# Layer 1 feed forward: every second gate and up block from the fifth on as seven block products, with all their sums and splits on DVE

## The chip, the cores and the metric

One NeuronCore of a Trainium2 chip runs the whole program. The metric is the device time of one execution in microseconds (us). The engines are PE (TensorE, matmuls; PEld is its weight load), DVE (VectorE), ACT (ScalarE), POOL (GpSimd) and SP (SyncE, which here issues the DMAs). Each engine executes its own instructions in a fixed order and waits on semaphores for the others.

## What is computed

A two-layer diffusion block on 512 latent tokens and 256 context tokens, width 1024. The change lies in the feed forward of the second layer (layer 1), which runs on the 512 latent tokens alone:

```python
def conv_ffn(h, w_up, conv_w, conv_b, w_down):
    g, u = jnp.split(h @ w_up, 2, axis=-1)
    g = dwconv(g, conv_w) + conv_b
    return (jax.nn.silu(g) * u) @ w_down
...
x_lat = x_lat + g1 * y_lat
x_lat = x_lat + g2 * conv_ffn(rmsnorm(x_lat, norm_ffn[layer]) * (1 + sc2) + sh2, *ffn_p[layer])
```

`w_up` is 1024 x 5632, that is 22 gate blocks and 22 up blocks of 128 columns; `w_down` is 2816 x 1024. `dwconv` is a convolution of three taps along the tokens.

## The kernel before

Activations lie transposed: 128 features on the partitions, tokens along the free axis. Every product is done in three passes of a rounded type: an operand is split into a high half (a cast on ACT) and a low half (source minus high, on DVE); this is `split` (lines 98 to 100). `gemm` (line 123) then issues for each of the 8 slices of the contraction high x high, high x low and low x high, and a matmul has its own weight load. A block f of the feed forward is one gate and one up block: 2 x 8 x 3 = 48 matmuls of 128x512.

`ffn` (line 1016) handles one block after the other, in groups of 8, 8 and 6 (`GROUPS`). For each block it loads the gate and up weights (`load_wk`: a DMA of 512 KB into a `raw` tile, a cast into `wh` on ACT, a subtraction into `wl` on DVE, each 128x1024), multiplies them into two PSUM tiles, and finishes with the convolution (`conv`, line 497: an ACT activation and two DVE instructions L96 of 128x511), Silu on ACT (L1041), the product with up (L93 on DVE) and a split. After a group come its eight down projections (`project`, line 929), the last group's through `passes` (line 939), which also prepares the final norm.

What sets the order: a scheduler places the instructions of each engine by the program's order, its own estimate of durations, and free buffers. The rings of buffers matter here: `raw`, `wh` and `wl` two buffers each, PSUM tiles `g` two buffers of 1024 columns (so the gate tile of block n+1 takes the buffer of the gate tile of block n, once the convolution has read it), `m` three, `t` five, `u` four, `ada` two. In block 1 the gate weights lie in slots of their own (`hold`), so that they can be split before block 0 is done.

Block 0 is multiplied in two halves of 256 tokens, because the norm before it (`norm_seg`, line 217 ff., with `norm_apply`) comes in two halves: per half and 8 slices it makes the high half on ACT and the low half on DVE (even slices) or POOL (odd slices), after a product of x with the scale, which reads PSUM.

Of the kernel before, what the change touches and what calls it, by code (L numbers as in the profile page):

```python
# [8 lines left out]
F32 = mybir.dt.float32  # L9
F32R = mybir.dt.float32r  # L10
# [40 lines left out]
def hybrid_kernel(ctx: ExitStack, tc: tile.TileContext, A, out):  # L51
# [204 lines left out]
    def ada_raw():  # L256
        return ap.tile([P, 1024], F32, tag="ada", name=nm("ada"))
# [681 lines left out]
    def passes(src, nk, mv, layer, which, segs, acc, norm):  # L939
        for m in range(KD - 2):  # L940
            project(load_wk(src(m), nk), mv, layer, which, m, segs, acc)
        w = [load_wk(src(m), nk) for m in (KD - 2, KD - 1)]
        apply = None
        for seg in segs:
            for i in range(2):
                project(w[i], mv, layer, which, KD - 2 + i, (seg,), acc)
            nxt = norm(seg)
            if apply:
                apply()
            apply = nxt  # L950
        return apply
# [334 lines left out]
            x[3 * i + k] = s[:, k, :]  # L1286
    acc = temp()[:, :NL]
    a, b = mod_ab(1, 1, "norm_ffn_1", 1)
    h = new_h((0, 1, 20, 21, 4, 6, 11, 15))
    apply = passes(lambda m: A["w_o"][m], KD, oh, 1, 0, HALF, acc, lambda seg: norm_seg(x, acc, a, b, h, seg))  # L1290
    acc2 = temp()[:, :NL]
    fn = vec("final_norm")

# [19 lines left out]

        return apply

    def tail_1(src, ng, acts):
        return passes(src, ng, acts, 1, 1, HALF, acc2, final)

    apply = ffn(1, h, zs, LAT, HALF, apply, tail_1, (7, 8, 9, 10, 18, 19, 16, 17, 5, 2), (18, 19))
    apply()  # L1320


# [146 lines left out]
```

## Time and profile before

| what | value |
|---|---|
| runs, median (lowest to highest) | 1777.81 us (1776.45 to 1781.27), 3 runs |
| the profiled execution | 1776.61 us |
| its span, first to last instruction | 1774.8 us |
| mean granted TensorE clock | 0.984 of full |
| PE / DVE / ACT / POOL busy | 97% / 61% / 37% / 11% of the span |
| the layer-1 feed forward, first matmul of block 0 to the last down projection | about 1384 to 1757 us |

The profiled execution lies 1.2 us under the median of the runs. 1.8 us of it are outside the span. Times in the rows are counted from the start of the span.

### The profile page before, as it was taken

What the parts mean: (1) busy time and instruction counts of PE and PEld (TensorE: products, weight loads), DVE (VectorE), ACT (ScalarE), POOL (GpSimd) and SP (SyncE); (2) the same over time, 40 slices, a digit from 0 to 9 for tenths busy, and PEclk for the clock granted to TensorE, in tenths of its full rate; (3) what the DMA queues carried; (4) which work ended last, traced back from release to release, by engine and by line L of the source; (5) the groups of instructions that cost most, each with busy time, mean ns of one, the idle gap of its engine ahead of it and who ended that gap; (6) DMA issues with size and microseconds to landing.
All of it is one profiled execution on the core that took longest, in us unless ns stands there. A gap on an engine that the chain in (4) does not pass through costs nothing.

```text
span 1774.8 us, 24363 instructions
## 1 busy us (share of the span) xinstructions
PE 1715.9 (97%) x9615; PEld 1439.0 (81%) x9615; DVE 1089.2 (61%) x1871; ACT 651.3 (37%) x1091; POOL 192.5 (11%) x193
## 2 busy tenths in 40 slices
PE   8899999998999999999999999989999999999997
PEld 2578887887888888888888888978888888888886
DVE  6777866739967457764355436487884644344445
ACT  4542332446543321132211324455553432232233
POOL 1551242015213000000000000000000300000001
PEclk9899999998999999999999999999999999999998
DMA  7156455312523134553255123110022223233322
GB/s 273 60 175 207 150 189 187 125 58 71 179 84 108 60 107 131 178 156 99 79 172 170 62 63 116 36 35 27 26 100 72 72 95 95 95 96 95 95 83 84
DMA packets 65668, 193.59 MB, mean 109 GB/s; under 512 B 7086, under 2 KB 17136, under 8 KB 65554
## 3 DMA queue, kind: packets, MB, share of 16 engines
q1 hardware_dynamic: 65554, 192.03, 33.5%
q8 instruction: 76, 1.25, 0.3%
q14 instruction: 38, 0.31, 0.1%
HBM read 178.37 MB, written 13.63 MB: 108 GB/s over the span
## 4 chain that ended last, share of the span: by engine, by line
PE 68%; DVE 4%; ACT 1%; POOL 1%; issue 1%; DVEq 0%; ACTq 0%; POOLq 0%
PE g L128 60%; PE g L1208 3%; PE m L128 1%; PE m L1226 1%; DVE t L93 1%; PE a L104 1%; PE a L103 1%; PE a L105 1%; DVE s L100 1%; DVE wl L100 0%; PE m L206 0%; PE a L128 0%; PE m L217 0%; POOL t L242 0%; PE a L321 0%
## 5 line engine op out<-in xcount | busy, mean ns | idle before, releaser
L128 PE MATMUL g<-s,wh 128*128 128x512 f32 (+1 forms) x4464 | 1077.7, 349 | 9.4 <-ACT s L241 3.6
L128 PEld LDWEIGHTS g<-s,wh 128*128 128x128 f32 x4464 | 727.5, 189 | 131.0 <-issue 6.6
L128 PE MATMUL g<-s,wl 128*128 128x512 f32 (+2 forms) x2232 | 655.4, 348 | 0.1
L99 ACT CAST wh<-raw 128x1024 fp32r<-128x1024 f32 (+4 forms) x219 | 213.4, 974 | 667.9 <-PE g L128 586.6
L128 PEld LDWEIGHTS g<-s,wl 128*128 128x128 f32 x2232 | 369.1, 189 | 58.0 <-DVE wl L100 0.6
L100 DVE TENSOR_TENSOR wl<-raw,wh 128x1024 fp32r<-128x1024 f32 (+4 forms) x219 | 251.0, 1148 | 232.8 <-ACT wh L99 227.6
L96 DVE SCALAR_TENSOR_TENSOR acc<-ada,sc,acc 128x512 f32<-128x512 f32 x224 | 164.9, 775 | 30.3 <-DMA ada<-in_ada_dram 28.8
L96 DVE SCALAR_TENSOR_TENSOR s<-g,mod,s 128x512 f32<-128x512 f32 (+1 forms) x102 | 62.5, 632 | 147.9 <-PE g L128 147.5
L96 DVE SCALAR_TENSOR_TENSOR t<-g,vecs,t 128x511 f32<-128x511 f32 x204 | 131.0, 642 | 26.5 <-ACT t L501 20.6
L93 DVE TENSOR_TENSOR t<-t,g 128x768 f32<-128x768 f32 (+2 forms) x52 | 41.3, 794 | 110.0 <-PE g L128 109.2
L501 ACT ACTIVATE t<-g,vecs 128x512 f32<-128x512 f32 x86 | 59.9, 696 | 79.4 <-DVE t L96 62.7
L242 POOL TENSOR_SCALAR t<-t,A,mod 128x256 f32<-128x256 f32 (+1 forms) x36 | 37.5, 1048 | 376.8 <-DVE t L93 372.8
L1208 PE MATMUL g<-s,s 128*128 128x512 f32 (+1 forms) x320 | 65.4, 347 | 3.7 <-DVE s L93 2.5
L1208 PEld LDWEIGHTS g<-s,s 128*128 128x128 f32 x320 | 49.3, 190 | 10.9 <-DVE s L93 4.1
L1041 ACT ACTIVATE t<-t 128x768 f32<-128x768 f32 (+1 forms) x42 | 31.1, 740 | 68.5 <-DVE t L96 68.5
L100 DVE TENSOR_TENSOR s<-m,s 128x512 fp32r<-128x512 f32 (+1 forms) x90 | 50.2, 588 | 8.3 <-ACT s L99 8.0
L99 ACT CAST s<-m 128x512 fp32r<-128x512 f32 (+1 forms) x90 | 42.5, 515 | 34.0 <-PE m L1226 24.1
L1308 POOL TENSOR_TENSOR s<-s,t 128x256 f32<-128x256 f32 x8 | 5.5, 728 | 363.1 <-ACT t L1304 363.1
L1151 POOL MEMSET s<- 64x768 f32 x1 | 0.7, 734 | 398.6 <-PE g L128 398.6
L199 ACT ACTIVATE t<-s 128x256 f32<-128x256 f32 (+2 forms) x58 | 31.4, 561 | 21.6 <-DVE s L96 18.1
L1217 ACT ACTIVATE u<-g,mx 128x768 f32<-128x768 f32 x32 | 28.9, 905 | 25.3 <-DVE mx L1215 23.0
L100 DVE TENSOR_TENSOR s<-t,s 128x768 fp32r<-128x768 f32 (+1 forms) x44 | 36.0, 818 | 0.0
(363 smaller groups left out, 1858.0 us busy)
## 6 DMA issues: line engine op xcount, KB each, us to landing
raw<-in_up_dram SPq DMA_DIRECT2D x88, 512.0 KB, 3.5
ada<-in_ada_dram SPq DMA_DIRECT2D x82, 512.0 KB, 3.7
raw<-in_down_dram SPq DMA_DIRECT2D x32, 512.0 KB, 3.6
raw<-in_w_in_dram SPq DMA_DIRECT2D x24, 512.0 KB, 4.5
raw<-in_w_out_dram SPq DMA_DIRECT2D x16, 512.0 KB, 3.4
s<-in_ada_dram SPq DMA_DIRECT2D x14, 512.0 KB, 7.9
s<-in_xT_dram SPq DMA_DIRECT2D x8, 768.0 KB, 5.5
raw<-in_down_dram SPq DMA_DIRECT2D x16, 384.0 KB, 3.2
```

Of the source, the lines that this page charges most:

```text
L93: return dve.tensor_tensor(o, a, b, op=op)
L96: return dve.scalar_tensor_tensor(o, a, s, b, op0=op0, op1=op1)
L99: act.copy(h, src)
L100: eng.tensor_tensor(l, src, f32(h), op=ALU.subtract)
L103: pe.matmul(o, s[0], m[0], start=start, stop=False)
L128: pe.matmul(ps[r][:, :n] if type(ps) is list else ps[:, lo:lo + n], w[a][:, k - k0, :], mv[k][b][:, lo:lo + n], start=first and k == ks[0] ...
L199: act.activation(sq, xa, AF.Square)
L242: pool.tensor_scalar(f[:, s], t[:, s], a[i], b[i], op0=ALU.mult, op1=ALU.add)
L501: act.activation(d, s, AF.Identity, scale=w[:, 1:2], bias=bias)
L1041: act.activation(t[:, :n], t[:, :n], AF.Silu, **({} if f else dict(bias=zs)))
L1208: pe.matmul(g[:, lo:lo + w_], s_, m_[:, lo:lo + w_], start=n == 0, stop=n == 4)
L1217: act.activation(pt, g[:, :T], AF.Exp, scale=MLA_SCALE, bias=mx, accum_out=sm)
```

## The change

Block 0 to 3, every odd block, 20 and 21 stay as they were, with 48 matmuls of 512 columns. Blocks 4, 6, 8, 10, 12, 14, 16 and 18 (eight of them) go through the new function `seven` (after.py, lines 1401 to 1442). The weights of up and gate form a 2 x 2 matrix of pieces (a11, a12 the two contraction halves of up; a21, a22 those of gate), and the activations one too (contraction halves by token halves of 256). Instead of eight products of pieces there are seven, each of 4 slices x 3 passes = 12 matmuls of 128x256. For that, four sums of weight pieces (`s1` to `s4`, 128x512 on DVE) are made per block; all seven weight operands are split from there (`wform`: cast of 128x512 on ACT, subtraction of 128x512 on DVE, in the buffers of `wh` and `wl`), and seven additions of 128x256 on DVE and one copy on ACT put gate and up together in SBUF. The raw weights come into the `ada` buffers.

Four sums of the activations are needed once for all blocks: `token_forms` computes them from the unsplit activations F (4 slices x 4 sums, 128x256 on DVE) and splits them (16 casts on ACT, 16 subtractions on DVE). So `norm_half` replaces `norm_seg`: it also writes F, on ACT for the even slices, on POOL for the odd ones.

```diff
-    h = new_h((0, 1, 20, 21, 4, 6, 11, 15))
-    apply = passes(lambda m: A["w_o"][m], KD, oh, 1, 0, HALF, acc, lambda seg: norm_seg(x, acc, a, b, h, seg))
+    us = [slot(i, [P, 6, NC], F32R) for i in (0, 1, 20, 21, 4, 6, 11, 15)]
...
+        def apply():
+            for k in range(KD):
+                t = temp()[:, :NC]
+                tt(t, x[k][:, s], g, ALU.mult)
+                hi, lo = B[k][j]
+                ak, bk = a[:, k, 0:1], b[:, k, 0:1]
+                act.activation(hi, t, AF.Identity, scale=ak, bias=bk)
+                if k % 2:
+                    pool.tensor_scalar(F[j][k], t, ak, bk, op0=ALU.mult, op1=ALU.add)
+                else:
+                    act.activation(F[j][k], t, AF.Identity, scale=ak, bias=bk)
+                (pool if k % 2 else dve).tensor_tensor(lo, F[j][k], f32(hi), op=ALU.subtract)
...
+    def token_forms():
+        for k in range(4):
+            f11, f12, f21, f22 = F[0][k], F[1][k], F[0][k + 4], F[1][k + 4]
+            t = temp()
+            t1, t2 = t[:, 0:NC], t[:, NC:2 * NC]
+            tt(t1, f12, f11, ALU.subtract)
+            tt(t2, f22, t1, ALU.subtract)
+            tt(f12, f22, f12, ALU.subtract)
+            tt(f21, f21, t2, ALU.subtract)
+            for n, v in enumerate((t1, t2, f12, f21)):
+                split(TF[n][k][0], TF[n][k][1], v)
...
-    apply = ffn(1, h, zs, LAT, HALF, apply, tail_1, (7, 8, 9, 10, 18, 19, 16, 17, 5, 2), (18, 19))
+    def wform(src, eng=dve):
+        t = wp.tile([P, 2, 512], F32R, tag=("wh", "wl")[turn[0] % 2], name=nm("wf"))
+        turn[0] += 1
+        split(t[:, 0, :], t[:, 1, :], src, eng)
+        return [t[:, i, :].rearrange("p (k m) -> p k m", m=P) for i in range(2)]
+
+    def seven(f):
...
+        tt(s1, a21, a22, ALU.add)
+        tt(s2, s1, a11, ALU.subtract)
+        product(p1, wform(a11), B11)
+        act.copy(q1, p1)
+        product(p6, wform(s2), T2)
+        tt(q6, p6, q1, ALU.add)
+        product(p5, wform(s1), T1)
+        tt(us_[:, hi], p5, q6, ALU.add)
+        product(p2, wform(a12), B21)
+        tt(us_[:, lo], p2, q1, ALU.add)
+        tt(s3, a11, a21, ALU.subtract)
+        product(p7, wform(s3), T3)
+        tt(q67, p7, q6, ALU.add)
+        tt(gs_[:, hi], p5, q67, ALU.add)
+        product(p4, wform(a22), T4)
+        tt(gs_[:, lo], p4, q67, ALU.add)
+        tt(s4, a12, s2, ALU.subtract)
+        product(p3, wform(s4), B22)
+        tt(us_[:, hi], us_[:, hi], p3, ALU.add)
+        gated(f, gs_, us_)
...
+    plain(wg, wu, gg, gu, (0, 1))
+    wu1 = load_wk(up[NF + 1], KD)
+    gated(0, gg, gu, zs)
+    token_forms()
...
+            if f % 2 or f in (2, 20):
...
+            else:
+                seven(f)
```

How the order moves, at the two places of which the prediction speaks. On DVE before, from the low half of block 1's up weights (`wl_1769`) to that of block 2's gate weights (`wl_1777`); the rows on `t_1763` and `t_1772` are the convolutions and products of blocks 0 and 1:

```order
L100 TENSOR_TENSOR wl_1769_12528<-raw_1767_12525,wh_1768_12527 128x1024
L96 SCALAR_TENSOR_TENSOR t_1763_12511<-g_1748_12372,vecs_84,t_1763_12511 128x511
L100 TENSOR_TENSOR wl_1777_12594<-raw_1775_12591,wh_1776_12593 128x1024
L96 SCALAR_TENSOR_TENSOR t_1763_12511<-g_1748_12372,vecs_84,t_1763_12511 128x511
L93 TENSOR_TENSOR t_1763_12511<-t_1763_12511,a_1749_12373 128x512
L96 SCALAR_TENSOR_TENSOR t_1772_12581<-g_1770_12531,vecs_84,t_1772_12581 128x511
L100 TENSOR_TENSOR s_1741_12359<-t_1763_12511,s_1740_12358 128x512
L96 SCALAR_TENSOR_TENSOR t_1772_12581<-g_1770_12531,vecs_84,t_1772_12581 128x511
```

One instruction stands between the two low halves. On DVE of the changed kernel, the last rows of the same stretch (`wl_1764` for block 1's up weights stands 37 rows ahead of `wl_1777`; `t_1770`, `s_1732`, `acc_1722` are the last slice of the token forms, `t_1773` the convolution of block 1):

```order
L93 TENSOR_TENSOR t_1770_12575<-s_1733_12323,t_1770_12575 128x256
L93 TENSOR_TENSOR s_1732_12322<-s_1733_12323,s_1732_12322 128x256
L93 TENSOR_TENSOR acc_1722_12242<-acc_1722_12242,t_1770_12575 128x256
L100 TENSOR_TENSOR s_1669_11934<-t_1770_12575,s_1669_11934 128x256
L100 TENSOR_TENSOR s_1673_11938<-t_1770_12575,s_1673_11938 128x256
L100 TENSOR_TENSOR s_1675_11940<-s_1732_12322,s_1675_11940 128x256
L100 TENSOR_TENSOR s_1676_11941<-acc_1722_12242,s_1676_11941 128x256
L96 SCALAR_TENSOR_TENSOR t_1773_12638<-g_1771_12588,vecs_84,t_1773_12638 128x511
L100 TENSOR_TENSOR wl_1777_12650<-raw_1775_12647,wh_1776_12649 128x1024
L96 SCALAR_TENSOR_TENSOR t_1773_12638<-g_1771_12588,vecs_84,t_1773_12638 128x511
```

Between the two low halves now stand 31 instructions of 256 columns (the token forms but one), two of 512 (product and split of block 0) and three halves of convolutions; the convolution of block 1 ends behind all of them.

On DVE of the changed kernel, the end of block 4 (`m_1804` and `g_1801` are the products p7 and p4, `u_1828` is `s1` of block 6, `wl_1819` the low half of block 5's gate weights):

```order
L93 TENSOR_TENSOR t_1805_12801<-m_1804_12800,t_1805_12801 128x256
L93 TENSOR_TENSOR t_1806_12802<-m_1802_12798,t_1805_12801 128x256
L93 TENSOR_TENSOR u_1828_13004<-ada_1827_13002 128x512
L93 TENSOR_TENSOR t_1806_12802<-g_1801_12797,t_1805_12801 128x256
L100 TENSOR_TENSOR wl_1819_12933<-raw_1817_12930,wh_1818_12932 128x1024
L96 SCALAR_TENSOR_TENSOR t_1815_12921<-t_1806_12802,vecs_84,t_1815_12921 128x511
```

The low half for block 5 stands behind two sums of block 4 and behind a sum for block 6, which needs a DMA. PE has at the same place (`wf_1813` is the weight operand of p4, `wf_1814` that of p3, `g_1823` block 5's gate):

```order
L128 MATMUL g_1801_12797<-s_1676_11941,wf_1813_12888 128x256 x6
L128 MATMUL g_1823_12942<-s_1666_11931,wh_1818_12932 128x512 x2
L128 MATMUL g_1801_12797<-s_1670_11935,wf_1814_12905 128x256 x3
L128 MATMUL g_1801_12797<-s_1671_11936,wf_1814_12905 128x256 x3
L128 MATMUL g_1801_12797<-s_1672_11937,wf_1814_12905 128x256 x3
L128 MATMUL g_1801_12797<-s_1673_11938,wf_1814_12905 128x256 x3
L128 MATMUL g_1823_12942<-s_1666_11931,wl_1819_12933 128x512
```

Only two matmuls of block 5 and the product p3 stand between p4 and the first matmul that needs the low half.

## Rows read from the trace of the kernel before

**Rows 1.** The page's head and part 1: span, busy time, share, instructions.
```profile
span 1774.8 us, 24363 instructions
...
PE 1715.9 (97%) x9615; PEld 1439.0 (81%) x9615; DVE 1089.2 (61%) x1871; ACT 651.3 (37%) x1091; POOL 192.5 (11%) x193
```

**Rows 2.** The chain that ended last: start us, us, what, times.
```profile
1377.12 3.78 PE g L128 x31
...
1399.17 0.36 PE g L128 x3
1399.53 0.35 PE a L128 x3
...
1402.27 354.28 PE g L128 x1548
```

**Rows 3.** Timeline of ACT in blocks 4 and 5: start, us, instruction, idle before.
```profile
1440.88 1.05 ACT L99 CAST wh<-raw 128x1024 fp32r<-128x1024 f32 x1 [3.93 <-PE g L128]
...
1452.04 1.05 ACT L99 CAST wh<-raw 128x1024 fp32r<-128x1024 f32 x1 [3.93 <-PE g L128]
```

**Rows 4.** Busy time by stretch: range, length, engines busy (instructions), PEclk, DMA share, GB/s.
```profile
1382.20:1386.60 4.40, 2.02 (x12) 1.58 (x12) 3.50 (x10) 3.50 (x6) 1.34 (x2) 1.00 0.29 106
1386.60:1393.40 6.80, 6.01 (x26) 5.72 (x27) 6.79 (x19) 2.80 (x6) 5.44 (x5) 0.50 0.42 130
1393.40:1402.30 8.90, 8.90 (x70) 8.37 (x69) 5.04 (x12) 4.60 (x10) 6.81 (x10) 1.00 0.05 20
1440.90:1463.20 22.30, 22.30 (x97) 18.02 (x96) 10.30 (x12) 8.00 (x10) 0.00 (x0) 1.00 0.29 94
```

**Rows 5.** Groups by form from 1340 us on: engine, shapes, count | busy us, mean ns.
```profile
L96 DVE SCALAR_TENSOR_TENSOR t<-g,vecs,t 128x511 f32<-128x511 f32 x44 | 32.8, 746 | 1.0 <-ACT t L501 0.3
...
L100 DVE TENSOR_TENSOR s<-t,s 128x512 fp32r<-128x512 f32 x22 | 15.1, 684 | 0.0
...
L99 ACT CAST s<-t 128x512 fp32r<-128x512 f32 x22 | 13.7, 621 | 0.2 <-DVE t L93 0.2
...
L128 PEld LDWEIGHTS g<-s,wh 128*128 128x128 f32 x1175 | 217.9, 189 | 48.5 <-DVE s L96 0.8 <-ACT s L227 0.7 <-POOL s L244 0.2
...
L200 DVE TENSOR_TENSOR t<-t,t 128x256 f32<-128x256 f32 x8 | 3.4, 424 | 2.9 <-ACT t L199 2.9
```

**Rows 6.** Timeline of DVE in the second norm half: two instructions of 256 columns.
```profile
1394.71 0.41 DVE L93 TENSOR_TENSOR t<-s,m 128x256 f32<-128x256 f32 x1
1395.04 0.47 DVE L96 SCALAR_TENSOR_TENSOR t<-s,A,m 128x256 f32<-128x256 f32 x1
```

**Rows 7.** DMA issues from 1402 to 1500 us: size, median us to landing.
```profile
raw<-in_up_dram SPq DMA_DIRECT2D x11, 512.0 KB, 3.4
```

**Rows 8.** Timeline of DVE behind block 0, as rows 6.
```profile
1402.97 1.23 DVE L100 TENSOR_TENSOR wl<-raw,wh 128x1024 fp32r<-128x1024 f32 x1 [3.62 <-ACT wh L99]
1404.11 0.74 DVE L96 SCALAR_TENSOR_TENSOR t<-g,vecs,t 128x511 f32<-128x511 f32 x1
1404.77 1.22 DVE L100 TENSOR_TENSOR wl<-raw,wh 128x1024 fp32r<-128x1024 f32 x1
...
1413.31 0.69 DVE L93 TENSOR_TENSOR t<-t,g 128x512 f32<-128x512 f32 x1 [2.83 <-PE g L128]
1414.10 1.23 DVE L100 TENSOR_TENSOR wl<-raw,wh 128x1024 fp32r<-128x1024 f32 x1
```

**Rows 9.** Busy time of PE alone by stretch, as rows 4, around two earlier waits.
```profile
411.40:414.70 3.30, 0.02 (x1) 0.87 0.42 104
414.70:420.70 6.00, 5.84 (x24) 0.50 0.44 162
...
425.20:427.30 2.10, 0.14 (x2) 1.00 0.00 0
427.30:430.90 3.60, 3.60 (x16) 0.53 0.00 0
```

More of the change, by code (lines that the diff above doesn't have):

```diff
@@ L1288, in hybrid_kernel @@
     a, b = mod_ab(1, 1, "norm_ffn_1", 1)
-    h = new_h((0, 1, 20, 21, 4, 6, 11, 15))
-    apply = passes(lambda m: A["w_o"][m], KD, oh, 1, 0, HALF, acc, lambda seg: norm_seg(x, acc, a, b, h, seg))
+    us = [slot(i, [P, 6, NC], F32R) for i in (0, 1, 20, 21, 4, 6, 11, 15)]
+    h = [(u[:, 0:2, :].rearrange("p a t -> p (a t)"), u[:, 2:4, :].rearrange("p a t -> p (a t)")) for u in us]
+    B = [[tuple(v[:, j * NC:(j + 1) * NC] for v in hk) for j in range(2)] for hk in h]
+    units = [(u[:, 4, :], u[:, 5, :]) for u in us]
@@ new lines, in hybrid_kernel, with norm_half @@
+    for i in (7, 8, 9):
+        u = slot(i, [P, 6, NC], F32R)
+        units += [(u[:, 2 * e, :], u[:, 2 * e + 1, :]) for e in range(3)]
+    TF = [[units[4 * n + k] for k in range(4)] for n in range(4)]
+    F = [None, None]
+    def norm_half(seg):
+        j = seg[0] // NC
+        s = slice(seg[0], seg[0] + NC)
+        g = norm_scale(acc[:, s], NC, D)[0][:, :NC]
+        if j:
+            fs = [slot(i, [P, 6, NC]) for i in (2, 3)]
+            F[1] = [fs[k // 6][:, k % 6, :] for k in range(KD)]
+        else:
+            f0, f1 = slot(10, [P, 6, NC]), ap.tile([P, 2, NC], F32, tag="acc", name=nm("acc"))
+            F[0] = [f0[:, k, :] if k < 6 else f1[:, k - 6, :] for k in range(KD)]
+        def apply():
[10 more added lines that the diff above has]
+                (pool if k % 2 else dve).tensor_tensor(lo, F[j][k], f32(hi), op=ALU.subtract)
+        return apply
@@ new lines, in token_forms @@
+    def token_forms():
[9 more added lines that the diff above has]
+                split(TF[n][k][0], TF[n][k][1], v)
+    apply = passes(lambda m: A["w_o"][m], KD, oh, 1, 0, HALF, acc, norm_half)
@@ L1314, in final, with act_unit @@
         return apply
-    def tail_1(src, ng, acts):
-        return passes(src, ng, acts, 1, 1, HALF, acc2, final)
-    apply = ffn(1, h, zs, LAT, HALF, apply, tail_1, (7, 8, 9, 10, 18, 19, 16, 17, 5, 2), (18, 19))
+    cw = vec("ffn_conv_w_1").rearrange("p (j w) -> p j w", w=3)
+    cb = vec("ffn_conv_b_1")
+    up, dn = A["up_1"], A["down_1"]
+    aslots = (16, 17, 5, 18, 19, 10, 2, 3)
+    acts, au = [], []
+    def act_unit(f):
+        o = []
+        for u in (2 * f, 2 * f + 1):
+            if u % 3 == 0:
+                au.append(slot(aslots[u // 3 % 8], [P, 3, NL], F32R))
+            o.append(au[u // 3][:, u % 3, :])
+        return o
@@ new lines, in gated, with plain @@
+    def gated(f, gate_ps, up_ps, bias=None):
+        t = temp()[:, :NL]
+        conv(gate_ps, cw[:, f, :], cb[:, f:f + 1], t, LAT)
+        act.activation(t, t, AF.Silu, **(dict(bias=bias) if bias is not None else {}))
+        tt(t, t, up_ps, ALU.mult)
+        o = act_unit(f)
+        split(o[0], o[1], t)
+        acts.append(o)
+    def plain(wg, wu, gg, gu, segs):
+        for j in segs:
+            mv = [B[k][j] for k in range(KD)]
+            o = slice(j * NC, (j + 1) * NC)
+            gemm_pair([gg[:, o]], wg, [gu[:, o]], wu, mv, ((0, NC),))
@@ new lines, in hybrid_kernel, with product @@
+    turn = [0]
+    def wform(src, eng=dve):
[4 more added lines that the diff above has]
+    def seven(f):
+        raws = []
+        for n in (NF + f, f):
+            r = ada_raw()
+            sync.dma_start(r, up[n].rearrange("p k m -> p (k m)"))
+            raws.append(r)
+        (a11, a12), (a21, a22) = ((r[:, 0:512], r[:, 512:1024]) for r in raws)
+        s1, s2, s3, s4 = (temp2()[:, :512] for _ in range(4))
+        ga_, gb_ = gtile(), gtile()
+        p1, p6, p4, p3 = (g[:, o:o + NC] for g in (ga_, gb_) for o in (0, 512))
+        p5, p2, p7 = (mtile()[:, :NC] for _ in range(3))
+        q = temp()
+        q1, q6, q67 = (q[:, i * NC:(i + 1) * NC] for i in range(3))
+        gs_ = temp()[:, :NL]
+        us_ = ap.tile([P, 512], F32, tag="acc", name=nm("acc"))
+        lo, hi = slice(0, NC), slice(NC, NL)
+        B11, B21, B22 = [B[k][0] for k in range(4)], [B[k][0] for k in range(4, 8)], [B[k][1] for k in range(4, 8)]
+        T1, T2, T3, T4 = TF
+        def product(ps, w, mv):
+            gemm([ps], w, mv, ((0, NC),))
+        tt(s1, a21, a22, ALU.add)
[18 more added lines that the diff above has]
+        gated(f, gs_, us_)
@@ new lines, in hybrid_kernel @@
+    wg, wu = load_wk(up[0], KD), load_wk(up[NF], KD)
+    wg1 = load_wk(up[1], KD, hold=(18, 19))
+    gg, gu = gtile(), atile()
+    apply()
+    plain(wg, wu, gg, gu, (0, 1))
+    wu1 = load_wk(up[NF + 1], KD)
+    gated(0, gg, gu, zs)
+    token_forms()
+    f0 = 0
+    for gi, ng in enumerate(GROUPS):
+        for f in range(max(f0, 1), f0 + ng):
+            if f % 2 or f in (2, 20):
+                wg, wu = (wg1, wu1) if f == 1 else (load_wk(up[f], KD), load_wk(up[NF + f], KD))
+                gg, gu = gtile(), gtile()
+                gemm(gg, wg, h, LAT)
+                gemm(gu, wu, h, LAT)
+                gated(f, gg, gu[:, :NL])
+            else:
+                seven(f)
+        mv = acts[f0:f0 + ng]
+        if gi < len(GROUPS) - 1:
+            for m in range(KD):
+                project(load_wk(dn[m][:, f0:f0 + ng, :], ng), mv, 1, 1, m, LAT)
+        else:
+            apply = passes(lambda m: dn[m][:, f0:f0 + ng, :], ng, mv, 1, 1, HALF, acc2, final)
+        f0 += ng
```

## The prediction

> **What bounds the kernel now.** I read the page's busy times first: PE is busy 97% of the span, DVE 61%, ACT 37% [rows 1]. A mean over stages says little, so the next view is the chain of waits, from the end backwards. In the feed forward of layer 1 it is one unbroken piece, PE alone for 354.28 us from 1402.27 on [rows 2]: nothing but the number and length of the matmuls sets the time there. The stretch of two whole blocks says the same: PE busy for all of 22.30 us at full clock, DVE 10.30 us, ACT 8.00 us [rows 4]. So there are 12.0 us of DVE and 14.3 us of ACT to spare per two blocks, and work that leaves PE is gained as long as PE never waits. Before that stretch lies one where PE does wait: the norm. [...]
>
> **The change part by part.** (a) *Matmuls.* The cast that opens a block comes at 1440.88 and at 1452.04 [rows 3], so a block takes 11.16 us, 0.2325 us for each of its 48 matmuls of 512 columns. Six matmuls of 256 columns, each with its own weight load, take 0.36 + 0.35 us [rows 2], 0.118 each; another piece has 31 of them in 3.78 us, 0.122. I take 0.118, measured in the same two-block kind of stream with every matmul recorded: 84 x 0.118 = 9.91 us for a short block. Gain 11.16 - 9.91 = 1.25 us, times eight: **-10.0 us**. Ends: 0.122 gives 10.25 and -7.3 us; exactly half of 0.2325 gives 9.77 and -11.1 us.
>
> [...]
>
> (b) *DVE and ACT in short blocks.* An instruction of 512 columns has 0.684 us [rows 5], but the next one begins sooner: 1.14 us after the start of one of 1024 columns that lasts 1.23, 0.66 after one of 511 [rows 8], 0.33 after one of 256 that lasts 0.41 [rows 6]; I take 0.61 for 512. A short block has 4 sums and 7 low halves of 512 (6.7 us), 7 additions of 256 (2.3) and the usual tail of two convolution halves, product and split (2.5): 11.5 us. A plain block has two low halves of 1024 (2.3) and the same tail: 4.8 us. Together 16.3 us of DVE beside 11.16 + 9.91 = 21.1 us of PE, so it fits by volume. ACT has seven casts of 0.62 us more [rows 5] and two of 1.05 less [rows 3], and fits as well.
>
> In order it is tight at one point. Let PE begin p1 of block 4 at 0. A product takes 1.4 us. Weight operands 1 and 2 are split during block 3, since two of the four buffers are free by then; operands 3 and 4 wait for its end, and follow the product of block 3 on DVE (0.7), so they are done at 1.3 and 1.9. The first four matmuls of p5, at 1.4, just find the former. Operand 6 needs the buffer of operand 2 (p6 ends at 3.3) and is done at 4.7; p7 ends at 7.1, p4 at 8.5. Reading operand 6 frees the raw weights for the DMA of block 6, which lands 3.4 us later [rows 7], at about 8.2; the sum s1 of block 6 waits for it and ends at 8.8; then one addition (9.2) and the low half of block 5 (10.4). PE wants that at 8.5 + two matmuls + p3 = 10.3. So PE waits some 0.1 to 0.5 us. In blocks 6, 10, 14 and 18 the order puts this low half ahead of the sum, and I find nothing to wait for. Four times 0.3: **+1.2 us**; ends 0, and 4 x 1.2 = 4.8 if the DMA takes a microsecond longer.
>
> (c) *The token forms, in block 1.* Here nothing covers the work. In the kernel before, DVE starts the low half of block 1's up weights at 1402.97, 0.70 us after block 0's last matmul at 1402.27 [rows 8, 2], since the cast needs a buffer that block 0 holds. In the changed order all but the first of the token forms' 32 instructions stand behind it, and behind them the convolution of block 1, whose two halves free the PSUM buffer for the gate of block 2. From 0.70 us after block 0: low half 1.14, 31 x 0.33 = 10.2, two of 512 1.2, three convolution halves 2.0, the low half for block 2 1.14, the last convolution half 0.75: 17.1 us after block 0. PE has done block 1 after 47 matmuls x 0.2325 = 10.9 us (before, it had at 1413.2: DVE's product begins at 1413.31 [rows 8]). So PE waits at least 6.2 us. On top, DVE waits for ACT a few times: ACT casts the up weights of block 2 only when block 1 is done (at 10.9, 1.05 us), and five casts of token forms stand behind that; instructions that need their predecessor start after its end and not 0.08 us before. I add 1.0 us: **+7.2 us**, ends 6.2 and 8.2.
>
> (d) *The clock.* [...] I take **+2.5 us**.
>
> (e) *The norm halves.* ACT gets 4 more instructions of 256 columns per half (some 2 us of ACT), DVE loses the fused forms, POOL keeps its number. The low half of block 0's up weights moves behind eight products on DVE, but 16 gate matmuls move ahead of it on PE. DVE also gets s1 and s2 of block 4 here (2 x 0.61). In the stretch from 1386.6 to 1393.4 DVE is busy 6.79 of 6.80 us [rows 4], so what is added there delays the second half; from 1393.4 on PE has 8.9 us of work as cover. I take **+0.5 us**, ends -1.5 (the gate matmuls that move ahead) and +2.0 (ACT's additional work).
>
> Sum: -10.0 + 1.2 + 7.2 + 2.5 + 0.5 = **+1.4 us**. The low ends add up to -4.6, the high ones to +10.7. The profiled execution, 1776.61 us, would become 1778.0; it lies 1.2 us under the median of the runs, so against the median I predict **1779.2 us**. A change of 0.3% (5.3 us) is about what a measurement of this kernel can tell from none.
>
> **The rivals.** *Block 2 hardly waits: faster.* If DVE got through the stretch of (c) in the 10.2 us that PE leaves it, (c) and (d) would fall away: -10.0 + 1.2 + 0.5 = -8.3, **1769.5 us**. It would take 39 instructions at a mean of 0.26 us in place of 0.42. Half of it, a wait of 3 us with little clock lost, would give -4. Against it: the 256-column rows have the same 0.41 to 0.42 us from two tiles in SBUF and from PSUM [rows 5, 6]. For it: only that the order could be met by instructions which run ahead in ways the old trace doesn't show. 0.12.
>
> *The short blocks wait: slower.* One mechanism: DVE takes s1 of the next short block ahead of the low half of the plain block, and s1 waits for a DMA. If that lands 4.6 us after its issue and not 3.4, PE waits 1.2 to 1.5 us at the end of every second short block; if the same delay also moves operands 3 to 6 behind PE, in each. The point is 1.25 us per short block: from there the gain of (a) is gone, and +10.2 us of (c), (d) and (e) are left: **1788 us**. For it: operands 3, 4 and 6 come within 0.1 to 0.4 us of their need. Against it: volume, 16.3 of 21.1 us. 0.20.
>
> *Weight loads show.* A load has 0.189 us [rows 5], more than 0.118; if a short matmul could not start sooner than a load lasts, a short block would take 84 x 0.189 = 15.9 us, +38 us for eight, with the rest **1827 us**. [...] The trace disagrees: 0.118 per matmul, each with its own load [rows 2]. 0.02.
>
> **How the numbers follow.** The forecast, that the wait in block 2 takes back what the short blocks gain, has 0.66. Its ends, 1773.2 and 1788.5 us, would need every term at the same end; its own range is 1774 to 1785, and 0.05 of the 0.66 lies above +5.3 us. So within 0.3%: 0.61 + 0.02 (half a wait, of the first rival) = 0.63. Faster: the other 0.10 of the first rival. Slower: 0.20 + 0.02 + 0.05 = 0.27. The range that should hold 8 in 10 goes from 1771 to 1788 us; outside stay most of the first rival and the upper part of the second.
>
> **What would show it.** Right: one wait of PE of 6 to 8 us before the first matmul of block 2, ended by DVE's L96 (the convolution of block 1), and a granted clock of 0.5 behind it; 12 matmuls of 256 columns in 1.42 us; no other PE wait over 0.5 us up to 1757; 288 more matmuls; DVE busy 60 to 80 us more. (a) is wrong if pairs take over 21.6 us; (c) if the wait is under 4 us or lies elsewhere; (d) if the clock stays at 1.0. Were short blocks not reached, the number of matmuls would stay.

## The result and the profile after

| | median of the runs | profiled execution | its span | stretch |
|---|---|---|---|---|
| before | 1777.45 us (1776.45 to 1781.27, 6 runs) | 1776.61 us | 1774.8 us | 374.3 us |
| after | 1787.14 us (1785.45 to 1790.93, 6 runs) | 1785.45 us | 1783.7 us | 382.6 us |

The medians differ by 9.7 us; the ratio on record is 1.0058, with a 95% interval of 1.0048 to 1.0068, so the changed kernel is slower. The range (1771 to 1788 us) held it, 0.9 us below its upper end; the most likely case did not: "within 0.3%" had 0.63, "slower" 0.27. "Stretch" is what the profiled executions are compared by from here on: from the last sum of the attention's output ahead of the norm (the L96 instruction of DVE of 0.48 us at 1382.22 before, 1382.79 after) to the first L206 of the final norm (1756.52 and 1765.36). What lies ahead of the norm does not change between these kernels and yet ended anywhere from 1379.9 to 1385.0 us in the profiled executions, so whole spans are a poor measure of a microsecond. The stretch grew by 8.3 us, 1.4 less than the medians; what follows places the 8.3.

The page of the kernel after, its head and part 1 [rows 1 for before]:

```profile
span 1783.7 us, 25157 instructions
...
PE 1713.6 (96%) x9903; PEld 1448.0 (81%) x9903; DVE 1153.9 (65%) x2031; ACT 679.3 (38%) x1163; POOL 192.7 (11%) x193
```

The 288 more matmuls and the 65 us more of DVE are there: the change does what it says. PE is busy 2.3 us less, in a span 8.9 us longer, so it waits. For what, the waits of PE from 1370 us on tell (in all, times, longest):

```profile
PE g L128 <- DVE t L96: 7.2, 1, 7.2
...
PE g L128 <- DVE t L93: 2.9, 4, 1.5
PE g L128 <- ACT s L1316: 1.9, 1, 1.9
PE g L128 <- POOL s L1321: 1.6, 3, 1.1
PE g L128 <- DVE s L1321: 1.0, 2, 0.7
...
PE g L128 <- ACT t L1426: 0.2, 1, 0.2
```

The first line is the wait before block 2, at the place, of the size and by the releaser forecast. What came behind it stands in the windows of the same trace (as rows 4): 7.3 us of almost nothing, 5.8 us at a granted clock of 0.50, then 0.99.

```profile
1415.30:1422.60 7.30, 0.10 (x1) 0.00 (x1) 6.88 (x17) 3.85 (x10) 0.00 (x0) 0.72 0.00 0
1422.60:1428.40 5.80, 5.77 (x14) 4.54 (x15) 2.31 (x3) 1.23 (x2) 0.00 (x0) 0.50 0.54 181
1428.40:1447.80 19.40, 19.40 (x84) 15.68 (x83) 7.84 (x10) 6.47 (x10) 0.00 (x0) 0.99 0.16 54
```

The second line, 2.9 us in four waits, is not the one forecast. The chain of waits shows where it comes from, here at the end of block 4 (the other three, from 1541, 1585 and 1674 us, read the same, with DMAs of 3.69, 4.55 and 3.64 us):

```profile
1452.89 0.11 DVE acc L93
1453.00 3.47 DMA ada<-in_up_dram
...
1456.50 0.30 DVE u L93
...
1457.11 0.43 DVE t L93
1457.54 0.04 issue
1457.58 12.47 PE g L128 x59
```

and the timelines of DVE and of PE at the same place:

```profile
1456.50 0.69 DVE L93 TENSOR_TENSOR u<-ada 128x512 f32<-128x512 f32 x1 [0.25 <-DMA ada<-in_up_dram]
1457.11 0.42 DVE L93 TENSOR_TENSOR t<-g,t 128x256 f32<-128x256 f32 x1
1457.44 1.22 DVE L100 TENSOR_TENSOR wl<-raw,wh 128x1024 fp32r<-128x1024 f32 x1
```

```profile
1455.16 1.57 PE L128 MATMUL g<-s,wf 128*128 128x256 f32 x12
1456.57 0.64 PE L128 MATMUL g<-s,wh 128*128 128x512 f32 x2
1457.58 1.69 PE L128 MATMUL g<-s,wf 128*128 128x256 f32 x12 [0.38 <-DVE t L93]
```

`u<-ada` is `s1` of block 6; it stands ahead of `t<-g,t`, the addition that reads p4. The twelve matmuls at 1457.58 are p3, and they start 0.04 us after that addition has ended: p3 lies in the same PSUM tile as p4.

A wait costs more here than the idle time that is listed. The two matmuls of 512 columns ahead of p3 need 2 x 0.2325 us, so p3 could have begun at 1457.04; it began 0.54 us later (0.38 are listed), and its twelve matmuls took 0.11 us longer than twelve in a stream (1.69 us, p4's 1.57). By the starts of the matmuls the four waits cost 4.0 us in place of the 2.9. The same count finds a second loss, in all eight short blocks: the first 72 matmuls of block 6 take 8.76 us (1469.77 to 1478.53), where 72 in a stream take 8.48, and the time is lost at the head of p6, which shares its tile with p1. That makes 2.4 us in the eight blocks; the waits list 0.2 us of it, the one piece ended by ACT's copy of p1 (L1426).

### The profile page after: what moved, and what is told of

Read it like the earlier page. It is cut to its first block, busy times and chain, and to the rows that moved or that the text cites. A ratio compares the mean times of both kernels' runs of the same rounds, so it can differ in the third digit from the quotient of the medians.

```text
span 1783.7 us, 25157 instructions
## 1 busy us (share of the span) xinstructions
PE 1713.6 (96%) x9903; PEld 1448.0 (81%) x9903; DVE 1153.9 (65%) x2031; ACT 679.3 (38%) x1163; POOL 192.7 (11%) x193
## 4 chain that ended last, share of the span: by engine, by line
PE 66%; DVE 4%; ACT 2%; issue 2%; POOL 1%; DMA 1%; DVEq 0%; ACTq 0%; POOLq 0%
PE g L128 56%; PE g L1208 2%; PE m L128 2%; PE m L1226 1%; DVE t L93 1%; DMA ada<-in_up_dram 1%; DVE s L100 1%; PE a L104 1%; PE a L103 1%; PE a L105 1%; DVE wl L100 0%; PE m L206 0%; POOL t L242 0%; PE m L217 0%; PE a L321 0%
## 5 line engine op out<-in xcount | busy, mean ns | idle before, releaser
L128 PE MATMUL g<-s,wh 128*128 128x512 f32 (+1 forms) x4208 | 1001.4, 348 | 20.6 <-DVE t L96 7.2
L128 PEld LDWEIGHTS g<-s,wh 128*128 128x128 f32 x4208 | 680.4, 189 | 131.6 <-issue 14.0
L128 PE MATMUL g<-s,wl 128*128 128x512 f32 (+2 forms) x2104 | 606.1, 346 | 0.1
L128 PEld LDWEIGHTS g<-s,wl 128*128 128x128 f32 x2104 | 346.1, 189 | 52.6 <-DVE wl L100 1.4
L100 DVE TENSOR_TENSOR wl<-raw,wh 128x1024 fp32r<-128x1024 f32 (+4 forms) x203 | 231.0, 1139 | 170.7 <-ACT wh L99 166.3
L96 DVE SCALAR_TENSOR_TENSOR acc<-ada,sc,acc 128x512 f32<-128x512 f32 x224 | 165.1, 776 | 30.7 <-DMA ada<-in_ada_dram 28.9
L96 DVE SCALAR_TENSOR_TENSOR s<-g,mod,s 128x512 f32<-128x512 f32 (+1 forms) x102 | 62.5, 633 | 147.9 <-PE g L128 147.7
L96 DVE SCALAR_TENSOR_TENSOR t<-g,vecs,t 128x511 f32<-128x511 f32 (+1 forms) x188 | 119.1, 633 | 26.8 <-ACT t L501 21.4
L93 DVE TENSOR_TENSOR t<-t,g 128x768 f32<-128x768 f32 (+2 forms) x44 | 35.8, 813 | 92.4 <-PE g L128 89.1
L501 ACT ACTIVATE t<-g,vecs 128x512 f32<-128x512 f32 x78 | 53.7, 688 | 80.9 <-DVE t L96 63.3
L128 PE MATMUL g<-s,wf 128*128 128x256 f32 x384 | 51.7, 284 | 3.1 <-DVE t L93 2.9
L128 PEld LDWEIGHTS g<-s,wf 128*128 128x128 f32 x384 | 48.1, 188 | 7.5 <-DVE t L93 4.6
L99 ACT CAST s<-t 128x768 fp32r<-128x768 f32 (+2 forms) x52 | 35.1, 678 | 21.3 <-DVE t L93 21.2
L1318 POOL TENSOR_SCALAR s<-t,A,mod 128x256 f32<-128x256 f32 x7 | 5.6, 793 | 334.3 <-ACT t L199 330.5
L100 DVE TENSOR_TENSOR s<-t,s 128x768 fp32r<-128x768 f32 (+2 forms) x52 | 39.2, 756 | 1.8 <-ACT s L99 1.8
```

Of the source, the lines that this page charges most:

```text
L96: return dve.scalar_tensor_tensor(o, a, s, b, op0=op0, op1=op1)
L128: pe.matmul(ps[r][:, :n] if type(ps) is list else ps[:, lo:lo + n], w[a][:, k - k0, :], mv[k][b][:, lo:lo + n], start=first and k == ks[0] ...
L1318: pool.tensor_scalar(F[j][k], t, ak, bk, op0=ALU.mult, op1=ALU.add)
```

## The experiments

All times are medians; "against before" is against the runs of the kernel before on the same chip. The ratio and its interval are those on record. The stretch is that of the one profiled execution.

| run | us | against before | ratio, 95% interval | stretch |
|---|---|---|---|---|
| after | 1787.14 | +9.7 | 1.0058 (1.0048 to 1.0068) | 382.6 |
| e1_pairs | 1785.52 | +7.8 | 1.0044 (1.0029 to 1.0059) | 382.6 |
| e2_s1pool | 1786.59 | +8.9 | 1.0047 (1.0032 to 1.0062) | 383.0 |
| e3_pairs_s1pool | 1790.19 | +12.5 | 1.0073 (1.0056 to 1.0089) | 387.8 |
| e4_tokens_pool | 1790.52 | +12.8 | 1.0080 (1.0063 to 1.0096) | 391.2 |
| e5_raw_first | 1786.44 | +10.0 | 1.0054 (1.0039 to 1.0069) | 385.0 |
| e6_tokens_spread | 1783.80 | +7.4 | 1.0041 (1.0026 to 1.0056) | 379.8 |
| e7_spread_norm | 1787.79 | +11.4 | 1.0064 (1.0049 to 1.0079) | 385.9 |
| e8_all_three | 1789.75 | +13.3 | 1.0073 (1.0056 to 1.0089) | 386.3 |
| e9_s1_after | 1782.22 | +4.2 | 1.0021 (1.0011 to 1.0031) | 377.2 |
| e10_tokens_even | 1775.97 | -2.1 | 0.9988 (0.9979 to 0.9998) | 375.9 |
| e11_norm_tail | 1785.83 | +7.8 | 1.0043 (1.0028 to 1.0058) | 383.1 |
| e12_both | 1771.96 | -6.7 | 0.9964 (0.9951 to 0.9978) | 368.6 |

**The short blocks: e1, e2, e3, e5, e9.** The question is what PE waits for at the end of a short block: the shared PSUM tile, the DMA ahead of the addition, or DVE as such.

e1, other pairs in PSUM:

```diff
-        p1, p6, p4, p3 = (g[:, o:o + NC] for g in (ga_, gb_) for o in (0, 512))
+        p1, p4, p6, p3 = (g[:, o:o + NC] for g in (ga_, gb_) for o in (0, 512))
```

> Edit: only the pairing of the products in PSUM changes (p1 with p4, p6 with p3, in place of p1 with p6, p4 with p3). Theory: in the changed kernel p3's first matmul waits until DVE has read p4 out of the same PSUM tile, and p6's until ACT has copied p1. With the new pairs both waits are gone from the head of p3 and p6; but the low half of the next plain block still stands behind s1 and its DMA, and PE needs it 1.4 us after p4, so part of the 2.9 us may come back there. So: no PE wait ended by DVE L93 before p3, and 1 to 4 us off the 9.7 us by which the changed kernel is slower than the kernel before (+6 to +9 against before). Rival (the tile is not the cause, s1 alone is): the waits move to the low half in full, and the time stays at +9.5 to +10.

The stretch did not change, but its parts did. The head of p6 is free now: the 84 matmuls of block 6 stand in one stream, 9.89 us from the first to block 7's first (likewise in blocks 10, 14 and 18):

```profile
1470.29 3.00 PE L128 MATMUL g<-s,wf 128*128 128x256 f32 x24
1473.13 4.41 PE L128 MATMUL m<-s,wf 128*128 128x256 f32 x36
1477.38 2.96 PE L128 MATMUL g<-s,wf 128*128 128x256 f32 x24
1480.18 0.63 PE L128 MATMUL g<-s,wh 128*128 128x512 f32 x2
```

The wait for the addition of p4 moved, from p3 to the next thing that needs it, and grew from 2.9 to 5.1 us in all: the gate of block 5 takes the buffer that p1 and p4 leave, and the low half now stands ahead of the addition as well. The chain at the end of block 4 in e1:

```profile
1452.51 3.90 DMA ada<-in_up_dram
...
1457.04 0.42 DVE t L93
1457.46 0.72 DVE wl L100
...
1458.51 0.43 DVE t L93
...
1459.07 14.22 PE g L128 x72
```

So p6's loss comes from the shared tile, but for the addition of p4 the tile decides only where PE waits; the DMA at the head of the chain stays. The median, +7.8, lies in the theory's range, the unchanged stretch speaks for the rival, and the interval holds both.

e2, `s1` on POOL:

```diff
-        tt(s1, a21, a22, ALU.add)
+        pool.tensor_tensor(s1, a21, a22, op=ALU.add)
```

> Edit: only s1, the first sum of a short block, moves from DVE to POOL, which is idle there. DVE no longer waits for the DMA of the raw weights of the next short block ahead of the last addition of p4. Theory (DMA ahead of the last addition, and the tile shared by p4 and p3): the four waits of together 2.9 us that DVE L93 ends before p3 fall to 0.1 or 0.2 us each, 2 to 3 us off: +6.5 to +8 against before. Rival (the shared tile alone, whatever DVE does first): each short block still waits for the addition, and the time falls by less than 1 us: +9 to +10.

The waits ended by L93 are gone, as the theory has it, and no DMA is left in the chain. The time, +8.9, lies between the two ranges, and its interval reaches into both. In place of those waits PE waits for the low half of the next plain block, which forms late because its cast waits for p7's weight buffer; and in the norm, where block 4's own `s1` now stands in POOL's queue, the wait for POOL grows from 1.6 to 3.2 us. Waits of PE from 1370 us on in e2:

```profile
PE g L128 <- POOL s L1321: 3.2, 2, 2.9
PE g L128 <- DVE wl L100: 2.1, 4, 0.5
```

e3 is e1 and e2 together.

> Both edits: new pairs in PSUM, and s1 on POOL. Theory: the eight short blocks lose neither the 5.0 us of blocks 4, 8, 12, 16 nor most of the 1.4 us of the others: 4 to 6 us off the changed kernel, +4 to +6 against before; the wait of 7.2 us before block 2 and the half clock behind it stay as they are. Rival (DVE and ACT are too late by volume, each operand a little): at most 2 us off, +8 or more, with the waits turned to the casts and low halves of the operands.

It was slower than either (+12.5, where +4 to +6 was expected), and no test of the theory: the order that came out of this edit has `s2` of the next block, which needs `s1` and so the DMA, on DVE ahead of the last addition. The same wait stood there in another guise (DVE L93: 5.2 us in four waits).

e5, the products of raw weights first (p1, p4, p2, then p6, p5, p7, p3), so that the raw tiles come free earlier:

> Edit: in the short blocks the three products whose weights come straight from the raw tiles go first (p1, p4, p2), then p6, p5, p7, p3; pairs in PSUM p1 with p4 and p6 with p3. So the raw tiles are read out some 5 us earlier, and the next short block's DMA is issued earlier. Theory (s1's DMA standing ahead of the last addition on DVE is what makes PE wait): no PE wait of over 0.3 us is left in the short blocks, the 5.0 us of blocks 4, 8, 12, 16 go: 3 to 5 us off the changed kernel, +5 to +7 against before. Rival (the ring of weight buffers is the limit: the cast for the next plain block waits until p7 has been read, as the 2.1 us ended by the low halves showed with s1 on POOL): waits of about 0.5 us each four times, only 1 to 2.5 us off, +7 to +9.

It missed as well (+10.0, where +5 to +7 was expected). The DMA is gone from the chain, but all four sums of the next block now come while this one's additions are due, and seven waits take the place of four:

```profile
PE g L128 <- DVE t L93: 4.7, 7, 0.8
```

e9 takes everything of the next block out of the way, with the new pairs of e1: `s1` is written into the tile that holds this block's gate sums, so it comes behind the convolution that reads them.

```diff
-        s1, s2, s3, s4 = (temp2()[:, :512] for _ in range(4))
+        if not xs2:
+            xs2.extend(temp2()[:, :512] for _ in range(2))
+        s1, gs_ = xs2[::-1] if f % 4 else xs2
+        s2, s3 = (temp2()[:, :512] for _ in range(2))
+        s4 = s2
...
-        p1, p6, p4, p3 = (g[:, o:o + NC] for g in (ga_, gb_) for o in (0, 512))
+        p1, p4, p6, p3 = (g[:, o:o + NC] for g in (ga_, gb_) for o in (0, 512))
```

> Edit: s1 of the next short block is written into the tile that holds the gate sums of this one, so that it can only come behind this block's convolution on DVE; s4 takes the tile of s2; and the pairs in PSUM are p1 with p4 and p6 with p3. So neither a DMA nor a sum of the next block stands ahead of the last additions, and p3 does not wait for p4's reading. Theory: both together are what the short blocks lose; no PE wait of over 0.2 us is left in them, 4 to 6 us off the changed kernel: +4 to +6 against before. Rival (DVE is too dense at the end of a short block in any order, as the run with the raw products first showed): the waits stay at 2 us or more in sum, and +7 to +9 is left.

That is the theory's number: +4.2, with a stretch 5.4 us shorter. The chain of e9 through block 4, block 5 and the start of block 6 is PE alone but for 0.02 us:

```profile
1453.06 4.25 PE m L128 x36
1457.31 2.80 PE g L128 x24
1460.11 0.02 issue
1460.13 14.23 PE g L128 x72
1474.36 4.25 PE m L128 x36
```

The window of one short and one plain block says the same:

```profile
1453.10:1474.40 21.30, 21.28 (x134) 18.96 (x133) 17.36 (x29) 10.30 (x17) 0.00 (x0) 1.00 0.31 103
```

DVE has 17.4 us of work in these 21.3 us. What the short blocks lost was order, not volume. The short blocks 6, 10, 14 and 18 take 9.89 us as in e1; in blocks 4, 8, 12 and 16 some 0.25 us is left, where the next gate begins just after the addition of p4 has ended. e1 has the same pairs, so what takes its 5.1 us of waits away is the new tiles of `s1`, `s4` and the gate sums, and the order that follows from them; these with the old pairs were not run.

**The token forms: e4, e6, e10.** e4 moves their 32 DVE instructions to POOL (in `token_forms`, `tt(...)` becomes `pool.tensor_tensor(...)`, and `split` gets `pool`).

> Edit: only the token forms' 16 sums and 16 low halves move from DVE to POOL, which does nothing between the norm and the end of the program. Theory: DVE's volume in block 1 makes the wait of 7.2 us before block 2, and the wait brings the half clock (2.9 us): both go, about 10 us off, -1 to +1 against before. POOL needs 32 x about 0.8 us = 26 us, until about 1430 us, and block 4 begins at about 1436 us. Rival 1 (POOL and DVE slow each other down, or POOL is late): a wait of 3 us or more before p6 of block 4, or longer DVE instructions in blocks 1 to 3, and +3 to +7. Rival 2 (the clock falls without the wait): 7 us off, +2.5.

Slower, and in the profiled execution, the slowest of its four (1796.11 us, the others up to 1790.79), the wait before block 2 grew to 12.9 us. The casts of the token forms stayed on ACT, and block 0's Silu and block 1's convolution stand behind casts in its order: from 1409.6 to 1425.5 us ACT waits for POOL ten times, 10.0 us in all. From ACT's timeline in e4:

```profile
1415.15 0.41 ACT L99 CAST s<-s 128x256 fp32r<-128x256 f32 x1 [0.98 <-POOL s L1333]
1415.46 0.72 ACT L1381 ACTIVATE t<-t,z 128x512 f32<-128x512 f32 x1
...
1425.46 0.40 ACT L99 CAST s<-acc 128x256 fp32r<-128x256 f32 x1 [0.28 <-POOL acc L1333]
1425.77 0.77 ACT L501 ACTIVATE t<-g,vecs 128x512 f32<-128x512 f32 x1
```

The casts of the token forms end at 1425.9; the convolution's activation (L501) follows them and ends at 1426.54. DVE's part of the convolution, which frees PE in the end, began at 1429.31 only: these last 2.8 us were DVE's, as the last section tells.

e6 leaves them on DVE and emits one slice in block 1, one in block 2, two in block 3.

> Edit: the token forms stay on DVE and ACT, but only one slice of the four is emitted in block 1; the second follows in block 2, the last two in block 3. Theory: it is their standing ahead of block 1's convolution that makes PE wait before block 2, not their volume: 24 x 0.335 = 8.0 us less stand there, the wait of 7.2 us and the 2.9 us at half clock go; 9 to 10 us off the changed kernel, -1 to +1 against before. Rival (volume): the wait moves to block 3 or 4, 2 us or more with a low clock behind it, and +3 to +7 is left.

The rival's picture came, and its number nearly (+7.4). The wait of 7.2 us is gone, but 3.2 us before a low half of block 3 came in its place, with the lower clock behind it (0.50 from 1433 to 1438 us), since in the order the two last slices stand ahead of block 3's low halves. Whether that is volume or order, e6 cannot tell; e10 can.

e10 puts one slice in each block, behind the request for that block's weights:

```diff
     apply()
+    token_forms(0)
     plain(wg, wu, gg, gu, (0, 1))
...
                 gemm(gu, wu, h, LAT)
+                if f < 4:
+                    token_forms(f)
                 gated(f, gg, gu[:, :NL])
```

> Edit: the token forms on DVE and ACT, one slice in each of four blocks: the first right behind the norm, the others after the weights of blocks 1, 2 and 3 have been asked for and ahead of those blocks' convolutions. Theory (order, not volume): neither the wait before block 2 nor the 3.2 us before a low half of block 3 that the earlier spread had in their place; no wait over 0.5 us from the end of block 0 to block 4 and the clock at 1.0: 9 to 11 us off the changed kernel, -1.5 to +1 against before. Rival (volume of DVE and ACT in blocks 1 to 3): waits of 2 us or more remain, +3 or more.

The same instructions on the same engines, and there is no wait from the end of block 0 to block 4 any more; the chain has PE alone there, for 155 matmuls:

```profile
1405.68 34.66 PE g L128 x155
```

From block 1's first matmul to block 4's first it takes 33.24 us (1405.52 to 1438.76), in the changed kernel 43.29 (1404.53 to 1447.82): 10.05 us less, and that is the 7.2 of (c) and the 2.9 of (d). All of it is the place of the token forms in the order. The median lies 11.8 us under the changed kernel's against before, a little more than was expected; the stretch of the profiled execution is only 6.7 us shorter. That execution was the slowest of its ten (1778.28 us): it lost some 1.3 us in block 12, where the clock was 0.61 (last section), and its norm took 1.5 us longer than the changed kernel's (see e11 and e12).

**The norm: e7, e11.** e7 is e6 with the fused forms of the kernel before in the norm, and F of the even slices put together afterwards by eight additions on POOL.

> As the run with spread token forms, and the norm's halves as in the kernel before (fused forms on DVE for the even slices); the unsplit activations of the even slices are put together again afterwards on POOL as high plus low half (8 additions of 256 columns, about 0.7 us each); the order of the slices is 1, 3, 0, 2. Theory: the 1.7 us lost up to the end of block 0 are the two more ACT instructions per slice and the POOL chain behind them: 1.5 to 2 us less than with the spread alone. Rival (they come from s1 and s2 of block 4, which stand among the norm's instructions on DVE, and from the order): no change to the spread alone, within 0.7 us.

It missed (+11.4), and shows why the norm is delicate: "afterwards" was only the program's order. On POOL the additions (L1330 in e7) were placed between the instructions of the second half, and PE then waits for POOL 7.0 us. e11 moves two low halves from POOL to DVE in the second half.

> Edit: in the norm's second half the low halves of the last two odd slices move from POOL to DVE, nothing else. Theory (the 1.7 us by which block 0 ends later come from POOL's chain of two instructions per odd slice in the second half): 0.8 to 1.7 us off, +8 to +9 against before. Rival (the two more ACT instructions per slice or the order on DVE): the wait is then ended by ACT or DVE, and the time stays within 0.5 us.

PE's waits for POOL fell from 1.6 to 1.1 us and for DVE from 1.0 to 0.7, POOL left the chain of the second half, and yet the stretch was 0.5 us longer; the intervals of the two ratios overlap. A window of the second half (as rows 4), first of the changed kernel, then of e11, then of e1:

```profile
1392.50:1397.00 4.50, 4.50 (x37) 4.31 (x37) 4.50 (x10) 1.28 (x3) 1.88 (x3) 1.00 0.39 131
```

```profile
1392.50:1397.00 4.50, 4.50 (x22) 4.50 (x23) 3.31 (x6) 0.10 (x1) 0.99 (x1) 0.50 0.40 130
```

```profile
1392.50:1397.00 4.50, 4.50 (x23) 4.50 (x23) 3.30 (x7) 0.39 (x1) 0.70 (x1) 0.50 0.45 157
```

In e11 the clock stayed at 0.50 to 1397 us, 22 matmuls in the time of 37. But so it did in e1, where PE, DVE, ACT and POOL have the same instructions in the same order as in the changed kernel, from the start of the stretch to block 1. So this need not come from e11's edit. With that one order the part from the start of the stretch to block 1's first matmul took 21.74 us in the changed kernel, where the clock was 1.00 from 1392.5 us on, and 21.76 in e6, whose chain through the norm has the same pieces; it took 22.86 in e1 and 22.83 in e5, where ten matmuls of 256 columns in a row took 2.1 us, 0.21 each (from 1392.85 and 1392.68 us; in the changed kernel 0.118). In e11 ten such took 2.13 us. Its 22.59 is to be compared with the latter two: a gain of some 0.25 us, not the 0.8 to 1.7 of the theory. What term (e) consists of stays open, and so does why the clock rose early in one execution and late in another.

e8 is e5 and e7 together.

> All three edits: raw products first, token forms spread, norm halves as before. Theory: the terms add up: +9.7 - 4 - 9.5 - 1.5 = about -5 against before (-3 to -8), the gain of the matmuls with little of it lost. Rival (each edit only moves its wait): within 3 us of the kernel before.

Two edits that had each only moved a wait did so together: +13.3, where -3 to -8 was expected.

**Both edits that helped: e12.**

> The edits of the two runs that took a wait away, together: s1 behind the convolution with the new pairs in PSUM, and one slice of the token forms in each of four blocks. Theory: the two waits lie in different stretches and add up: the changed kernel's +9.7, less 5.5 and less 11.8 as those two runs measured, is -7.6 us against before; range -5 to -9.5. What is then left of the -10 forecast for the matmuls is lost in the norm (about 2 us). Rival (PE's time is given back elsewhere, by a new wait or the clock): -1 to -4.

The terms add up: 6.7 us faster than the kernel before, where 7.6 was expected, and faster than both kernels. In the trace PE waits for nothing between block 0 and the final norm but 0.02 or 0.03 us at four places; of the waits that are left from 1370 us on, the norm ahead of block 0 has

```profile
PE g L128 <- DVE s L1321: 1.9, 3, 1.1
PE g L128 <- ACT s L1316: 1.9, 1, 1.9
PE g L128 <- POOL s L1321: 1.7, 2, 1.1
```

The stretch is 5.7 us shorter than before: 9.1 behind block 1's first matmul are gained, 3.4 in the norm are lost (23.28 us in place of 19.89). In e1, where the clock rises as late (ten matmuls in a row 2.14 us, in e12 2.13), the norm takes 22.86 us, so the order of e12 costs some 0.4 us of these 3.4: in its chain two sums of the first token slice (`s` L93) stand on DVE ahead of the norm's last low half, for which PE waits.

```profile
1403.29 1.40 DVE s L93 x2
1404.69 0.89 DVE s L1321
```

## Why the prediction was right, and where it was wrong

The stretch grew by 8.3 us where the terms gave +1.4. Term by term:

| term | forecast | found | from |
|---|---|---|---|
| (a) matmuls | -10.0 (-7.3 to -11.1) | -10.2 | e1 and e9: a short block without a wait takes 9.89 us; 8 x (11.16 - 9.89) |
| (b) end of the short blocks | +1.2 (0 to 4.8) | +6.5 | by the starts of the matmuls: 4.0 at p3 in blocks 4, 8, 12, 16, 2.4 at p6 in all eight, 0.1 in smaller pieces |
| (c) wait before block 2 | +7.2 (6.2 to 8.2) | +7.2 | the wait; with (d) 10.05, from the 43.29 us of blocks 1 to 3 and the 33.24 of e10 |
| (d) clock | +2.5 (1.8 to 3.0) | +2.9 | block 2's first 14 matmuls at 0.50: 6.11 us (1422.63 to 1428.74), at 0.2325 each 3.26 |
| (e) norm halves | +0.5 (-1.5 to 2.0) | +1.9 | from the start of the stretch to block 1's first matmul: 21.74 (1404.53 - 1382.79), before 19.89 (1402.11 - 1382.22) |

The five add up to the 8.3, each found by itself.

*Right: (a), (c) and (d).* (c) came by its mechanism and to the tenth: counting 39 instructions of DVE by their distance in a stream gave the wait. (d) came too, 0.4 us larger. Its +2.5 was my estimate, half of the 3.6 to 6.0 us for which the clock of [rows 9] stayed at 0.53 and 0.50. That a matmul takes twice as long there no run shows: in the changed kernel one of 512 columns took 0.427 us at 0.50, in place of 0.2325, and block 2's first fourteen lost 2.9 us. Of the 1.0 us added for DVE's waits for ACT 0.42 was needed, one wait at 1416.17. In (a) the rate of 0.118 held. The sign that was named for a wrong (a), pairs of over 21.6 us, did come: a short and a plain block of the changed kernel take 21.3 to 23.0 us. But the surplus is (b)'s, as e9 shows, in which such a pair takes 21.30 at most. The rival "weight loads show" fell as expected: 36 matmuls of 256 columns take 4.25 us in e9, 0.118 each, every one with its own load; in the changed kernel such a load (of `wf`) takes 0.188 us.

*Wrong: (b), the step "PE waits some 0.1 to 0.5 us" and "I find nothing to wait for" in blocks 6, 10, 14, 18.* The cause was named, a sum of the next short block that waits for a DMA on DVE ahead of what PE needs. But I let PE run on to the low half, 1.9 us after p4, and took only that for its limit. The addition of p4, one row ahead in the order, was needed sooner: p3 starts in the PSUM tile from which it reads. That took p3's 1.4 us of slack away. And the DMA took 3.5 to 4.6 us, not the 3.4 of the row, which is for the other blocks' raw tiles [rows 7]. That p6 shares its tile with p1, which ACT copies, is nowhere in the working; it cost 2.4 us. So (b) lies beyond the upper end of its range. This is the mechanism of the rival "the short blocks wait", at 0.8 us a block: less than the 1.25 us from which that rival was to decide, so not the case as written.

*Too small: (e).* "From 1393.4 on PE has 8.9 us of work as cover" failed: in the first half already PE waits 1.1 us for POOL, and the second is paced by POOL, not by PE (the chain of waits has POOL L1318 and L1321 from 1396.2 to 1402.4 us). With the clock's late rise, as in e1 (0.50 to 1397 us), the same order gives +3.0, above the range. Whether that is behind some of the 1.4 us by which the medians differ more than the stretches is not shown.

Of the error of 6.9 us in the stretch (b) makes 5.3, (e) 1.4, (d) 0.4, and (a) takes 0.2 off. That the range held the time all the same was in part luck: its upper part stood for an end of -7.3 in (a), which was not needed, and for a rival that came at two thirds of its size.

## What to carry to other kernels

Count what stands ahead of an instruction on its in-order queue, not the volume of the queue: the same instructions on the same engines gave +9.7 us in one order and -6.7 in another (with other tiles for a few of them). Work of a later stage that becomes ready early is the danger, above all when it waits for a DMA; a dependence that keeps it behind the present stage's last read (here, sharing a tile) removed 5.1 us of waits but for 0.25 us at four places. In e4, moving such work to an idle engine did not help while part of it (the casts on ACT) stayed in a queue that others need. For a prediction: follow, at the tightest place, every consumer of the late instruction, the first one that shares a tile with it included. And before an edit is blamed for a change of a microsecond, look whether the clock took the same course: the same norm took 21.7 or 22.9 us.

## What the runs showed of the hardware

**One DVE instruction of 512 columns took 8.44 us** in e4, against 0.684 us [rows 5]:

```profile
1416.22 0.69 DVE L93 TENSOR_TENSOR t<-t,a 128x512 f32<-128x512 f32 x1 [5.13 <-ACT t L1381]
1420.94 8.44 DVE L100 TENSOR_TENSOR s<-t,s 128x512 fp32r<-128x512 f32 x1 [4.04 <-ACT s L99]
```

It ended at 1429.38, just after POOL's last instruction of the token forms (1428.12 + 0.72 us, the end of a row without a gap). The L93 before it, which reads one operand from PSUM, ran beside the same POOL stream at its usual length (0.69 us; 0.68 in the changed kernel). Eleven POOL instructions in a row began while the long one ran; why it took so long the trace does not show. It stands alone: in the traces of the kernel before and of the changed kernel a DVE instruction beside POOL's took at most 1.6 us longer than usual (2.34 us in place of 0.75, at 152.8 us in the kernel before). How often it happens in e4 no trace shows: the other runs of e4 took 1789.88 to 1790.79 us, this one 1796.11.

**Waits of 1.4 to 1.8 us did or did not cost the clock.** After 1.45 us of waiting in block 12 of the changed kernel p3's twelve matmuls took 1.69 us, after 1.82 us in e10 2.89 us:

```profile
1590.28 1.69 PE L128 MATMUL g<-s,wf 128*128 128x256 f32 x12 [1.45 <-DVE t L93]
```

```profile
1581.64 2.89 PE L128 MATMUL g<-s,wf 128*128 128x256 f32 x12 [1.82 <-DVE t L93]
```

In the first the granted clock stayed at 1.00, in the second it was 0.61 on average from 1581 to 1584.2 us and 0.88 to 1588. In e3 a wait of 1.4 us in block 4 was followed by 0.80 (1461 to 1464.4 us) and 0.90 (to 1475). So the wait of 1.45 us cost 0.1 us on top, the one of 1.82 us some 1.3 us (2.89 against 1.57 for twelve matmuls that did not wait).
